# A hybrid decoder step on one core: the first mixer's scan in 8 chunks of 64 tokens instead of 16 of 32

## The chip, the cores and the metric

The kernel runs on one core of a Trainium2 chip. The metric is the device time of one execution in microseconds (us), the median of several runs. The core's engines work side by side, each through its own queue of instructions, and wait for one another on semaphores: PE (TensorE, the matrix multiplications; PEld is its loading of weights), DVE (VectorE), ACT (ScalarE), POOL (GpSimd), and SP (SyncE), which here issues the DMA transfers.

## The reference, cut to what matters

One inference step of a two-layer trunk, for a prompt of 512 new tokens and a sample group of 8 sequences with 4 new tokens each (32 tokens): 544 columns in all. Layer 0 mixes with an RG-LRU and an RWKV-7 side by side, layer 1 with HGRN2, and each is followed by a SwiGLU FFN. The change concerns RWKV-7 alone, which has 8 heads of size 64:

```python
def _rwkv_step(S, inp):
    r_t, w_t, k_t, v_t, kk_t, a_t = inp
    sk = jnp.einsum('bhvk,bhk->bhv', S, kk_t)
    S = (S * w_t[:, :, None, :] - sk[..., None] * (kk_t * a_t)[:, :, None, :]
         + v_t[..., None] * k_t[:, :, None, :])
    return S, jnp.einsum('bhvk,bhk->bhv', S, r_t)
...
    S_T, o = lax.scan(_rwkv_step, S0.astype(F32),
                      (tm(r4), tm(hd(decay)), tm(k4), tm(v4), tm(kk), tm(hd(a))))
    mean = jnp.mean(o, axis=-1, keepdims=True)
    var = jnp.mean(jnp.square(o - mean), axis=-1, keepdims=True)
    on = ((o - mean) * lax.rsqrt(var + GN_EPS)).reshape(B, T, W_B) * lnx_w + lnx_b
    bonus = (jnp.sum(r4 * k4 * r_k, axis=-1, keepdims=True) * v4).reshape(B, T, W_B)
    return (on + bonus) * g, S_T, pb[:, -1]
```

Each token changes a 64x64 state per head by what the token before left, so the step over tokens is a chain. It can be cut into chunks: within a chunk of C tokens the corrections U of all tokens follow from a triangular system of C rows, (I - N) U = rhs, where N holds the products of keys and decayed keys within the chunk and rhs the part that comes from the values V and from the state at the chunk's start. What passes from chunk to chunk is the state alone.

## The kernel before, in words

**The whole.** The program runs mixer 0, its output projection, FFN 0, mixer 1 (HGRN2), its output projection and FFN 1, one after the other. The dense products split each fp32 weight into a high and a low part, `wh` (made by ACT, L202) and `wl` (made by DVE or POOL, L205), and take three products per weight tile on halves of 272 columns. All matrix products go through the helper `mm` (L171), which is why most PE rows of the profile name that line; the tile's name tells them apart (`acc` is a dense product, `ch` the chain of the scan).

**RWKV-7 in chunks of 32.** `NCH` is 16 chunks, `p` counts 4 pairs of heads, `par` the two heads of a pair. `front` and `back` (L542 to L589) make the decayed keys and values factors: `KB` holds both key factors of a chunk (32 columns for V, 32 for U) and `W` the query factors (`al` for the state's part of rhs, the receptance for the output). `scores` (L528) multiplies KB with W, masks the result, and stores it in the other 64 partitions of W: after that one column block of W stacks 64 rows for the state, 32 for V and 32 for U, and one product of 128 rows does all three. The tile `Z` stacks the state S, V and U in the same way. `keys` (L678 to L695) scales KB to KH, turns it with TensorE transposes (tile `tmps`) and ACT copies it to `TM`, which carries V and U to the next state.

**The inverse.** `couple` (L599 to L611) computes N for all chunks, and sends it through DRAM (`nd_p`, the sample's in `nd_s`) so that one partition holds one 32-row block. DVE inverts the two 16-row halves of each block by forward substitution in 15 steps of two instructions (L653, L655). The result Y goes to DRAM (`y_p`) and a transposed copy too (`z_p`), and 16 DMAs bring them back as `Yt` and `Zt` (L670). `join` (L790, L793) builds the lower left quarter of each 32-row block from these with two products per block (tile `jps`), for four chunks at a time.

**The chain.** `scan` (from L803) does per chunk: rhs from W and Z (8 products, tile `ch`), a DVE copy (L827); U from Yt and rhs (8 products), four DVE copies into Z (L842); the new state from TM and Z (8 products), two DVE adds with the decayed state `sp` (L850; `sp` is POOL's, L831); and 8 products for the outputs. The three numbers of `HOP=(8,7,7)` are how many products of other work are placed on PE behind each of these three steps. That other work is the RG-LRU's input projections and gates (L991 to L1050), later the first columns of the output projection (`lead`).

**What sets the order.** The string `MID` orders the last part of the preparation (`a`/`A` and `b`/`B` the two halves of `keys`, `r`/`R` of `receptance`, `x` the values, `g` the output gate). The string `PLAN` orders the scan: `c` a chunk, `s` a stage of the sample group (`sample`, L913 to L985: a scan of its own for the 32 sample tokens, with state products `rpss`, `opss`, `dpss`), `g` and `h` the two halves of the group norm of a block of 128 tokens (L874 to L907), `f` so many products of other work. From the step `r3` on, PE executes in exactly that written order. The queues of the other engines are set when the program is built, by a scheduler with the priorities that the code gives.

```python
    def fill(self, n):
        while n and self.work:
            try:
                next(self.work[0])
                n -= 1
```

Of the kernel before, what the change touches and what calls it, by code (L numbers as in the profile page):

```python
# [30 lines left out]
CH = 32  # L31
HB = CH // 2
NCH = SEQ // CH
EPS = 1e-6
# [17 lines left out]
MID = 'v0 v2 v3 a3 v1 A3 b3 a1 r3 B3 A1 b1 a2 r0 R3 B1 A2 x b2 a0 x r1 x B2 R0 A0 x b0 r2 x R1 B0 g R2'  # L52
# [29 lines left out]
def consts_np():  # L82
# [30 lines left out]
    c["smask"] = np.stack([pair(True), pair(False)], 1)  # L113
    c["upper"] = np.tile((np.arange(CH) < CH // 2)[:, None], (4, 1)).astype(np.float32)
# [14 lines left out]
class Build:  # L129
# [205 lines left out]
    def mixer0(self):  # L335
# [90 lines left out]
        smask = const("smask", [128, 2, 2, 64])  # L426
        upper = const("upper", [128, 1])
        seqsel = const("seqsel", [128, 8])
        block64 = const("block64", [128, 128])
        g2 = const("g2", [128, 512], kp)  # L430

        NC1 = NCH + 1
        W = [[m0.tile([128, NC1, 64], F32, name=f"W{par}{p}") for p in range(4)] for par in range(2)]
        TM = [m0.tile([128, NC1, 64], F32, name=f"TM{p}") for p in range(4)]
# [4 lines left out]
        Yt = m0.tile([128, NCH, 2, CH], F32, name="Yt")  # L439
        Zt = m0.tile([128, NCH, 2, CH], F32, name="Zt")  # L440
        NTt = m0.tile([128, 2, NCH, CH], F32, name="NTt")
        Yts = m0.tile([64, 4, CH], F32, name="Yts")
        sg = kp.tile([128, NT], F32, name="sg")
        nd_p = self.dr.tile([8, NCH, CH, CH], F32, name="nd_p")
        nd_s = self.dr.tile([8, CH, CH], F32, name="nd_s")
        vT = self.dr.tile([NT, 4, 128], F32, name="vT")
        y_p = self.dr.tile([8, NCH, CH, CH], F32, name="y_p")
        z_p = self.dr.tile([8, NCH, CH, CH], F32, name="z_p")
        y_s = self.dr.tile([8, CH, CH], F32, name="y_s")
        par_rows = (slice(0, 64), slice(64, 128))  # L450
        sc_rows = (slice(64, 128), slice(0, 64))
        VS, US = [slice(CH, 64), slice(0, CH)] * 2, [slice(0, CH), slice(CH, 64)] * 2
# [4 lines left out]

        def chunks(z):
            return z.rearrange("p (c t) -> p c t", t=CH)
# [40 lines left out]
        f2 = self.open("feat2")  # L500
        eb = [f2.tile([128, NT + 1], F32, name=f"eb{p}") for p in range(4)]
        KB = [f2.tile([128, NC1, 64], F32, name=f"KB{p}") for p in range(4)]
# [13 lines left out]
        def quarter(c):  # L516
            return slice(32 * (c % 4), 32 * (c % 4) + 32)

        def scores(p):
            for c0, cn in ((0, 8), (8, 8), (16, 1)):  # L520
                ps = self.ms.tile([128, 8, 64], F32, tag="m", name="scps")
                for c in range(c0, c0 + cn):
                    for par in range(2):
                        r = par_rows[par]
                        self.mm(ps[sc_rows[par], c - c0], KB[p][r, c], W[par][p][r, c])
                for par in range(2):
                    sr = sc_rows[par]
                    TT(W[par][p][sr, c0:c0 + cn], ps[sr, 0:cn],  # L528
                       smask[sr, p % 2, c0 // 16, None, :].to_broadcast([64, cn, 64]), OP.mult)
# [27 lines left out]
        def back(p, kap):  # L557
# [23 lines left out]
            E("kb")(KB[p][:, :, VS[p]], chunks(km), chunks(emb), OP.mult)  # L581
            STT(ta, ta, 1.0, kap, op0=OP.add, op1=OP.mult)
            STT(KB[p][:, :, US[p]], chunks(ta), -0.5, chunks(emb), op0=OP.mult, op1=OP.mult)
            for par in range(2):
                r = par_rows[par]
                al = W[par][p][r, :, 0:CH]
                E(f"al{par}")(al, chunks(kap[r]), chunks(eb[p][r, 0:NT]), OP.mult)
                nc.gpsimd.tensor_copy(al[:, 0:NCH, 0:1], kap[r, 0:SEQ:CH][:, :, None])
                nc.gpsimd.tensor_copy(al[:, NCH, 0:CH:NS], kap[r, SEQ::NS])  # L589
# [1098 lines left out]
```

## Time and profile before

| | |
|---|---|
| median of 3 runs | 1540.97 us (1539.78 to 1542.6) |
| profiled execution | 1541.22 us, its span 1539.4 us |
| granted TensorE clock, mean | 0.971 |
| PE busy | 1465.2 us, 95% of the span |
| DVE, ACT, POOL busy | 860.2 us, 552.5 us, 418.3 us |
| mixer 0's preparation and scan | from the start to about 345 us |
| PE idle between 100 and 340 us | 50.5 us (240 us less the busy time of twelve windows of 20 us) |

The profile names engines, lines and tiles: a row of the timeline gives the start in us, the duration, the engine, the line, the operation, output<-input by the program's names, the shape, how many instructions are merged in the row, and in brackets the idle time before it with what ended it. A row of the windows gives for each stretch its length, the busy time of PE, PEld, DVE, ACT and POOL with their numbers of instructions, the granted clock (1.00 is full speed), the share of the DMA engines and GB/s. A row of the waits gives who waited, for whom, and the total us, the number of waits and the longest. A plain fp32 product stands as two instructions on PE: eight products of the program are a row with x16.

### The profile page before, as it was taken

The numbers are of one execution on the slowest core, as the hardware profiler recorded it, in microseconds if no ns is written. First come the engines' busy times: TensorE is split into PE (matmuls) and PEld (weight loads), VectorE is DVE, ScalarE is ACT, GpSimd is POOL, SyncE is SP. The second block draws the span as 40 slices with busy tenths as digits, with TensorE's granted clock in tenths as the row PEclk, the third lists the DMA queues.
The fourth block names the chain that finished last, engine by engine and source line by source line (L and its number), as shares of the span: only waits on it lengthen the run. The fifth ranks groups of instructions, "written<-read, shape, count | busy, mean of one in ns | idle before, by whom it ended". The sixth has DMA issues, their size and how long they took to land.

```text
span 1539.4 us, 33537 instructions
## 1 busy us (share of the span) xinstructions
PE 1465.2 (95%) x13872; PEld 1408.7 (92%) x13872; DVE 860.2 (56%) x1618; ACT 552.5 (36%) x997; POOL 418.3 (27%) x540
## 2 busy tenths in 40 slices
PE   6967888779999999999999999999999999999998
PEld 6857777669999999999999999999999999999997
DVE  7777555785544344334576667666674433444444
ACT  5634234354433233223352333333453322332224
POOL 3664535542110011001133434444431100110010
PEclk9978989889999999999999999999999999999999
DMA  4224311122232322322231232322242222223221
GB/s 158 70 71 104 105 38 36 49 80 93 83 96 83 90 89 84 96 83 91 85 120 58 85 98 85 106 87 90 97 124 90 89 86 87 90 90 90 84 75 59
DMA packets 92010, 133.86 MB, mean 87 GB/s; under 512 B 28976, under 2 KB 34864, under 8 KB 91728
## 3 DMA queue, kind: packets, MB, share of 16 engines
q1 hardware_dynamic: 91856, 131.71, 27.2%
q8 instruction: 109, 1.79, 0.5%
q14 instruction: 45, 0.37, 0.1%
HBM read 120.65 MB, written 11.02 MB: 86 GB/s over the span
## 4 chain that ended last, share of the span: by engine, by line
PE 84%; DVE 7%; ACT 3%; issue 2%; DMA 2%; POOL 1%; SPq 1%; DVEq 0%; POOLq 0%; ACTq 0%
PE acc L171 74%; PE lv L171 2%; PE ops L171 1%; PE ch L171 1%; DVE Z L842 1%; DVE t L571 0%; PE ds L171 0%; PE tr L1503 0%; DVE W L528 0%; PE nps L171 0%; DVE wl L205 0%; DMA S<-rS 0%; DMA x<-xT 0%; DMA wd<-down 0%; DVE Pd L653 0%
## 5 line engine op out<-in xcount | busy, mean ns | idle before, releaser
L171 PE MATMUL acc<-xg,wh 128*128 128x272 f32 x4544 | 888.1, 293 | 11.7 <-ACT xg L262 7.2
L171 PEld LDWEIGHTS acc<-xg,wh 128*128 128x128 f32 x4544 | 721.7, 191 | 21.7 <-ACT xg L262 7.5
L171 PE MATMUL acc<-xg,wl 128*128 128x272 f32 x2272 | 653.1, 293 | 0.2 <-DVE wl L205 0.2
L202 ACT ACTIVATE wh<-wf 128x512 fp32r<-128x512 f32 (+1 forms) x404 | 250.8, 621 | 655.8 <-PE acc L171 544.3
L171 PEld LDWEIGHTS acc<-xg,wl 128*128 128x128 f32 x2272 | 429.1, 190 | 4.9 <-issue 1.3
L205 DVE TENSOR_TENSOR wl<-wf,wh 128x512 fp32r<-128x512 f32 (+1 forms) x373 | 267.1, 716 | 192.2 <-ACT wh L202 166.2
L1207 POOL TENSOR_TENSOR S<-S,rstd 128x272 f32<-128x272 f32 x88 | 74.3, 845 | 645.3 <-ACT S L1206 645.2
L171 PE MATMUL acc<-h,wh 128*128 128x272 f32 x1280 | 236.9, 288 | 0.0
L171 PEld LDWEIGHTS acc<-h,wh 128*128 128x128 f32 x1280 | 198.0, 188 | 0.0
L171 PE MATMUL acc<-h,wl 128*128 128x272 f32 x640 | 176.7, 287 | 0.0
L171 PEld LDWEIGHTS acc<-h,wl 128*128 128x128 f32 x640 | 118.1, 188 | 0.0
L1210 DVE TENSOR_TENSOR hh<-acc,S 128x272 f32<-128x272 f32 x88 | 38.9, 442 | 127.2 <-PE acc L171 125.3
L171 PE MATMUL acc<-cat,wh 128*128 128x272 f32 (+2 forms) x512 | 100.2, 295 | 2.7 <-ACT wh L202 2.7
L171 PEld LDWEIGHTS acc<-cat,wh 128*128 128x128 f32 x512 | 82.7, 194 | 3.5 <-ACT wh L202 3.1
L1206 ACT ACTIVATE S<-t 128x272 f32<-128x272 f32 x88 | 37.8, 431 | 123.4 <-DVE t L1205 123.4
L1227 DVE TENSOR_TENSOR x<-acc,x 128x272 f32<-128x272 f32 x80 | 35.0, 439 | 83.3 <-PE acc L171 83.0
L1205 DVE TENSOR_TENSOR t<-acc,rstd 128x272 f32<-128x272 f32 x88 | 38.7, 441 | 70.7 <-PE acc L171 70.6
L171 PE MATMUL acc<-cat,wl 128*128 128x272 f32 (+2 forms) x256 | 74.2, 296 | 2.0 <-POOL wl L205 1.0
L280 POOL TENSOR_TENSOR ssq<-ssq,sq 128x544 f32<-128x544 f32 x33 | 46.5, 1410 | 93.4 <-ACT sq L279 93.0
L1477 POOL TENSOR_TENSOR K<-K,G 128x256 f32<-128x256 f32 (+1 forms) x48 | 39.8, 828 | 78.3 <-PE lv L171 78.3
L205 POOL TENSOR_TENSOR wl<-wf,wh 128x512 fp32r<-128x512 f32 x31 | 41.3, 1334 | 40.7 <-ACT wh L202 40.4
L171 PEld LDWEIGHTS acc<-cat,wl 128*128 128x128 f32 x256 | 49.2, 194 | 2.8 <-POOL wl L205 1.4
(341 smaller groups left out, 1506.9 us busy)
## 6 DMA issues: line engine op xcount, KB each, us to landing
wf<-gate SPq DMA_DIRECT2D x88, 256.0 KB
wf<-up SPq DMA_DIRECT2D x88, 256.0 KB
wf<-down SPq DMA_DIRECT2D x72, 256.0 KB
wf<-w_in_c SPq DMA_DIRECT2D x64, 256.0 KB
wf<-w_in_ab SPq DMA_DIRECT2D x44, 256.0 KB
x<-xT SPq DMA_DIRECT2D x16, 272.0 KB
wf<-w_out_ab SPq DMA_DIRECT2D x16, 256.0 KB
S<-hS SPq DMA_DIRECT2D x8, 512.0 KB
```

The source lines that it names most:

```text
L171: return self.seq(self.nc.tensor.matmul(out, lhsT, rhs, start=start, stop=stop, skip_group_check=True), chain)
L202: nc.scalar.activation(wh[:, :n], wf[:, :n], AF.Copy)
L205: eng.tensor_tensor(wl[:, :n], wf[:, :n], wh[:, :n].bitcast(F32), OP.subtract)
L280: eng.tensor_tensor(self.ssq, self.ssq, t, OP.add)
L842: nc.vector.tensor_copy(zc[par][q, e::2], cu[q])
L1205: nc.vector.tensor_tensor(t[:, c], ps, rs()[:, c], OP.mult)
L1206: nc.scalar.activation(S[:, c], t[:, c], AF.Silu)
L1207: nc.gpsimd.tensor_tensor(S[:, c], S[:, c], rs()[:, c], OP.mult)
L1210: nc.vector.tensor_tensor(hh[:, c], ps, S[:, c], OP.mult)
L1227: nc.vector.tensor_tensor(x[:, c], ps, x[:, c], OP.add)
L1477: PTT(kv[:, :, 0], kv[:, :, 0], g2[:, :, 1, None].to_broadcast([128, m, b]), OP.mult)
```

## The change

**What it does.** The chunk has 64 tokens instead of 32, so there are 8 chunks instead of 16.

- The stacked tiles go. `W`, `KB`, `TM`, the new `SV` (masked scores for V in the output) and the state `S`, `V`, `U` hold two heads each, one in partitions 0 to 63 and one in 64 to 127, and every product of the chain is 64x64 on one of the two diagonal quadrants of the PE array. What was one product of 128 rows is up to three of 64 rows, added up in PSUM. The masked scores for rhs take the place of KB's first half.
- Per chunk the chain has three steps as before: rhs (8 products with S; the 8 with V stand in the chunk before) and one DVE copy; U (8 products with `T`, the inverse, added to rhs in the same PSUM bank) and one DVE copy; the new state (8 products with U; the 8 with V stand ahead) and one DVE add. 24 products give the outputs. `HOP` is (18,18,18).
- The inverse of 16-row halves stays on DVE. It goes to DRAM as Y alone (the transposed copy and `z_p` go), and 16 DMAs bring it back into the block diagonal of `T`, which POOL has set to zero. `join` then works in two levels, 16 to 32 rows and 32 to 64 rows, in four steps for each group of four chunks; the first group stands in `MID` (four `j`), the second in `PLAN` (`j1` four times).
- `keys` makes one KH of 128x512 for V and one for U, with two buffers, and turns them with 64x64 products against the identity (`turn`) instead of 128x128 transposes; so does the group norm with the outputs.
- The sample's scan keeps blocks of 32 and gets its own tiles (`Ws`, `KBs`, `TMs`). Its stages are now called in groups of three and four (`s3`, `s4` in `PLAN`).
- The pool of the inverse's tiles is opened before the features instead of after them, in other memory.

```diff
-CH = 32
-HB = CH // 2
+CH = 64
+CB = 32
+HB = CB // 2
...
-PLAN = 's1 f30 c1 c1 s1 c1 s1 c1 s1 c1 s1 g0 c1 s1 c1 s1 c1 h0 s1 c1 s1 c1 s1 s1 c1 c1 s1 g1 c1 s1 c1 s1 c1 h1 g2 s1 c1 s1 l3 c1 c1 h2 f20 d0'
+PLAN = 'c1 j1 f12 j1 f8 c1 j1 f4 j1 s1 c1 s1 g0 c1 s3 h0 c1 s4 g1 c1 h1 s4 c1 s3 g2 l3 c1 c1 h2 f20 d0'
...
-HOP = (8, 7, 7)
+HOP = (18, 18, 18)
+KHB = 2
+MIDJ = 4
...
+        iv = self.open("inv", side="right")
+        NTt = iv.tile([128, 4, NCH, CH], F32, name="NTt")
+        Ns = iv.tile([128, CB, CB], F32, name="Ns")
+        Y = iv.tile([128, CB, CB], F32, name="Y")
+        f2 = self.open("feat2", side="right")
...
-            ACT(Zc, Y.rearrange("p i t -> p t i"), AF.Copy)
...
+            for p in range(4):
+                for par in range(2):
+                    for half in range(2):
+                        nc.sync.dma_start(T[quarter(par, half), :, p, CB * half:CB * half + CB],
+                                          y_p[2 * p + par, half::2].rearrange("c i t -> i c t"))
...
+        def turn(out, src):
+            for par in range(2):
+                r = par_rows[par]
+                self.mm(out[r], src[r], ident[r, r])
...
+        def heads(out, w, src, start, stop):
+            for p in range(4):
+                for par in range(2):
+                    r = par_rows[par]
+                    self.mm(out[r, p], w(p)[r], src[r, p], start=start and p == 0, stop=stop, chain=True)
+
+        def outputs(c, V, S, U, ops):
+            for p in range(4):
+                terms = [(SV[p][:, c], V), (W[p][:, c, CH:], S), (KB[p][:, 1, c], U)]
+                if c == 0:
+                    terms.pop(1)
+                for i, (w, x) in enumerate(terms):
+                    for r in par_rows:
+                        self.mm(ops[r, c % 2, p], w[r], x[r, p], start=i == 0, stop=i == len(terms) - 1, chain=True)
...
+                    else:
+                        heads(cr, lambda p: W[p][:, c, 0:CH], S, False, True)
                     nc.vector.tensor_copy(rhs, cr)
+                    heads(cs, lambda p: TM[p][:, 0, c], V, True, False)
...
+                    for p in range(4):
+                        for r in par_rows:
+                            self.mm(cr[r, p], T[r, c, p], rhs[r, p], start=False, stop=True, chain=True)
+                    nc.vector.tensor_copy(U, cr)
                 self.fill(HOP[1])
                 with first():
+                    heads(cs, lambda p: TM[p][:, 1, c], U, False, True)
...
+                    if c + 1 < NCH:
+                        inputs(c + 1)
+                    outputs(c, V, S, U, ops)
```

**How it moves instructions.** On POOL, at the end of the feature preparation, the rows around the first `KH` before are these (`zero` is the tile that clears the sample's block in DRAM, `Y` the inverse's start, `X` the shifted projection):

```order
L476 TENSOR_TENSOR d<-X 128x544
L477 TENSOR_TENSOR d<-shift,X 128x8
L635 MEMSET zero 32x256
L645 MEMSET Y 128x1024
L645 MEMSET Y_1041 64x16
L678 TENSOR_TENSOR KH<-KB_278,ebT 128x512
L681 TENSOR_TENSOR KHs<-KB_278,ebT 128x64
```

and with the change, where the memsets of `zero` and `Y` stand at the very start of the program:

```order
L605 TENSOR_TENSOR bonus<-t_909,bonus 128x544
L617 COPY Ws_258<-kap 64x8
L478 MEMSET X 128x1
L607 TENSOR_TENSOR KBs_262<-bonus,t_924 128x32
L713 TENSOR_TENSOR KHs<-KBs_262,ebT 128x64
L710 TENSOR_TENSOR KH<-KB_250,ebT 128x512 x2
L485 COPY shift_sb<-X 128x9
```

Nothing of the inverse stands ahead of `KH` on POOL any more, and the two KH of a head pair follow one another.

On PE, the end of the sample's scan (`opss` its outputs, `tps` the turned outputs after the group norm, `gps` the output gate, `dpss` its new state). Before, 82 rows of chunks and other work stand between the last `opss` and its `tps`:

```order
L171 MATMUL acc<-xg,wl 128x272
L171 MATMUL acc<-xg,wh 128x272
L895 MATMUL tps<-ident,o 128x32 x4
L171 MATMUL gps<-sg,g_237 128x32 x4
L171 MATMUL ch<-Z_2133,W_239 32x64
L171 MATMUL ch<-Z_2137,W_243 32x64
```

With the change they follow directly, and the later `dpss` of three head pairs stand one behind the other in the same way:

```order
L179 MATMUL opss<-S_3039,am_3044 32x64 x16
L179 MATMUL opss<-Zs_3049,Ws_254 32x64
L179 MATMUL opss<-Zs_3050,Ws_258 32x64
L973 MATMUL tps<-ident,o 128x32 x4
L179 MATMUL gps<-sg,g_241 128x32 x4
L179 MATMUL dpss<-vx,TMs_263 64x512 x2
L179 MATMUL ch<-S,W_243 64x64 x2
```

On DVE, in the middle of the scan (`st`, `o` and `q` are the group norm's, `cf`, `uc`, `ti`, `tr` and `v` the RG-LRU's). Before, these rows stand between one rhs copy and the copies of U into Z, and between these and the adds of the state:

```order
L827 COPY rhs<-ch 128x128
L879 TENSOR_REDUCE st_2830<-q 128x8
L996 TENSOR_TENSOR UX<-acc,rstd 128x240
L998 TENSOR_TENSOR UX<-acc,rstd 128x8x4
L1042 SCALAR_TENSOR_TENSOR tr<-uc,ti 128x544
L881 TENSOR_SCALAR st_2830<-st_2830 128x8
L842 COPY Z_2130<-ch 32x2x64
L842 COPY Z_2134<-ch 32x2x64
```

With the change 29 rows stand between the add of the state of chunk 3 and the copy of rhs of chunk 4, of which these are the last:

```order
L1095 SCALAR_TENSOR_TENSOR uc<-UX,vec,cf 128x512
L1097 SCALAR_TENSOR_TENSOR uc<-UX,vec,cf 128x32
L965 SCALAR_TENSOR_TENSOR st_3780<-st_3780 128x8
L1127 SCALAR_TENSOR_TENSOR v_268<-a,tr 128x544
L963 TENSOR_TENSOR st_3780<-st_3780 128x8
L964 SCALAR_TENSOR_TENSOR st_3780<-st_3780 128x8
L965 SCALAR_TENSOR_TENSOR st_3780<-st_3780 128x8
L963 TENSOR_TENSOR st_3780<-st_3780 128x8
L964 SCALAR_TENSOR_TENSOR st_3780<-st_3780 128x8
L965 SCALAR_TENSOR_TENSOR st_3780<-st_3780 128x8
L907 COPY rhs<-ch 128x256
L917 COPY U<-ch 128x256
```

The work between two copies of the chain is more, and the copies themselves are fewer: 24 instead of 112.

More of the change, by code (lines that the diff above doesn't have):

```diff
@@ L30 @@
 FT = DFF // 128
-CH = 32
-HB = CH // 2
+CH = 64
+CB = 32
+HB = CB // 2
 NCH = SEQ // CH
+NCB = SEQ // CB
 EPS = 1e-6
@@ L683, in keys @@
                         ebT[:, p, NCH:][:, None, :, None].to_broadcast([128, 2, NB, NS]), OP.mult)
             yield
-            ps = self.ms.tile([128, 4, 128], F32, tag="m", name="tmps")
-            for c in range(4):
-                self.seq(nc.tensor.transpose(ps[:, c], KH[:, 2 * c:2 * c + 2].rearrange("p c t -> p (c t)"), ident))
-            for odd in range(2):
-                for par in range(2):
-                    ACT(TM[p][sc_rows[par], c0 + odd:c0 + 8:2], ps[par_rows[odd], :, par_rows[par]], AF.Copy)
@@ L691, in keys @@
-            if half:
+            ps = self.ms.tile([128, NCH, CH], F32, tag="m", name="tmps")
+            for c in range(NCH):
+                turn(ps[:, c], KH[:, c])
+            ACT(TM[p][:, w], ps, AF.Copy)
+            if w:
                 ps = self.ms.tile([64, 128], F32, tag="m", name="tmps")
@@ L731, in mixer0 @@
+        jp = self.open("joins", side="right")
+        joins = itertools.chain(join(0), join(1))
         parts = {}
@@ L763, in mixer0, with load_v, load_vs @@
         self.ms = ms
-        def copy(par, out, src):
-            if par:
-                ACT(out, src, AF.Copy)
-            else:
-                nc.vector.tensor_copy(out, src)
-        def load_v(c, zc):
+        def load_v(c):
+            V = z.tile([128, 4, 64], F32, tag="V", name="V", bufs=nv)
+            for par in range(2):
+                r = par_rows[par]
+                nc.sync.dma_start(V[r], vT[CH * c:CH * c + CH, :, r])
+            return V
+        def load_vs(zc):
             for par in range(2):
@@ L805, in scan, with inputs @@
         def scan():
-            ops = None
-            def slot(c):
-                return [Z[0][c % nz], Z[1][c % nz]]
+            ops = S = None
+            Vs = {}
+            def inputs(c):
+                heads(cr, lambda p: KB[p][:, 0, c], Vs[c], True, c == 0)
             with first():
-                for c in range(nz - 1):
-                    load_v(c, slot(c))
+                for c in range(nv - 1):
+                    Vs[c] = load_v(c)
             yield
-            with first():
-                join(0, 0)
@@ L909, in sample @@
         def sample():
+            for _ in joins:
+                pass
+            if MIDJ < 8:
+                self.close("joins")
             self.close("inv")
@@ L913, in sample @@
             nc.sync.dma_start(S0, I["rS"])
-            am = [sm.tile([128, NB, CH], F32, name=f"am{i}") for i in range(4)]
+            am = [sm.tile([128, NB, CB], F32, name=f"am{i}") for i in range(4)]
             for i in range(4):
@@ L1098, in mixer0 @@
                 self.fill(n)
+            elif k == "j":
+                for _ in range(n):
+                    next(joins, None)
             elif k == "l":
```

345 lines of the change are left out of this document (188 added, 157 removed).

## The prediction

> **What bounds the kernel now.** I read the page first, then the chain, the windows, the waits of PE, and last the timelines at its longest waits. The change stays within mixer 0. Columns of the windows: length, busy time of PE, PEld, DVE, ACT and POOL, granted clock, DMA share, GB/s.
>
> ```profile
> PE 84%; DVE 7%; ACT 3%; issue 2%; DMA 2%; POOL 1%; SPq 1%; DVEq 0%; POOLq 0%; ACTq 0%
> ...
> 100.00:120.00 20.00, 6.24 (x148) 4.93 (x148) 12.35 (x24) 5.55 (x15) 13.38 (x22) 0.57 0.30 83
> 180.00:200.00 20.00, 14.64 (x331) 12.60 (x331) 8.93 (x21) 2.15 (x4) 6.07 (x11) 0.83 0.36 120
> 220.00:240.00 20.00, 17.40 (x288) 14.69 (x288) 13.80 (x41) 4.24 (x9) 10.24 (x15) 0.66 0.08 21
> 260.00:280.00 20.00, 15.19 (x294) 12.87 (x291) 16.39 (x41) 4.73 (x7) 9.48 (x11) 0.83 0.09 23
> 300.00:320.00 20.00, 15.23 (x196) 11.57 (x192) 17.61 (x33) 8.71 (x17) 12.56 (x14) 0.91 0.15 47
> 360.00:380.00 20.00, 20.00 (x157) 20.00 (x156) 11.94 (x16) 9.50 (x15) 6.33 (x4) 1.00 0.09 29
> ```
>
> From 360 us on PE is full at full clock: nothing is to be had there. In mixer 0 it has holes and loses clock: 6.24 busy us at 0.57 before the scan, 15 to 17 us of 20 in the scan. So the time is PE's work in mixer 0, plus what it waits, plus what slow stretches cost. The waits (total, number, longest):
>
> ```profile
> PE ch L171 <- DVE Z L842: 13.9, 11, 3.4
> PE tmps L687 <- POOL KH L678: 10.1, 4, 7.4
> PE rpss L171 <- DMA S<-rS: 3.7, 1, 3.7
> PE tmps L687 <- DVE W L528: 3.6, 1, 3.6
> PE ch L171 <- DVE rhs L827: 3.0, 3, 1.5
> PE tps L895 <- POOL o L889: 1.8, 1, 1.8
> PE tmps L693 <- DVE W L528: 1.4, 2, 1.0
> PE ch L171 <- DVE Z L850: 1.2, 1, 1.2
> ```
>
> The chain waits for DVE 18.1 us (13.9, 3.0, 1.2), the turning of KH for POOL and DVE 15.1 us, the sample's first product for its state 3.7 us.
>
> **A. PE's own work.** One price carries most: 68 instructions (34 products) of 64x64 took 2.20 us, 64.7 ns each.
>
> ```profile
> 147.24 2.20 PE L171 MATMUL scps<-W,KB 64*64 64x64 f32 x68
> 146.60 0.60 PE L687 MATMUL tmps<-ident,KH 128*128 128x128 f32 x4
> 179.99 0.43 PE L171 MATMUL ch<-Z,W 128*32 128x64 f32 x16
> 180.35 0.73 PE L171 MATMUL jps<-Yt,NTt 32*32 32x16 f32 x64
> 105.11 1.77 PE L171 MATMUL ndps<-KB,W 64*32 64x32 f32 x116 [0.30 <-POOL W L588]
> 240.45 0.39 PE L171 MATMUL acc<-xg,wh 128*128 128x272 f32 x1
> 241.83 0.68 PE L171 MATMUL ch<-Z,TM 64*64 64x64 f32 x16 [0.24 <-DVE Z L842]
> ```
>
> - KH turned by 16 products, 1.04 us, instead of a row of 0.60: +0.44, 8 times, +3.5 us. The outputs' turns likewise, 4 times: +1.7.
> - Scores: per pair 16 products of 128 columns at twice the price (2.07) and 18 of 64 (1.16), 3.23 for 2.20: +1.0, 4 times, +4.1. Coupling: +0.2.
> - Joins: 8 rows of 0.73, 5.8 us, become 512 products. At this row's 22.8 ns they take 11.7 us; with half of them, those with 32 columns, at 30.5 ns (1.77 over 58 products, at a clock of 0.50, so an upper bound) 13.6. I take the row of the same shape: +5.8; the other end is +7.8.
> - Chain: 16 times 0.43+0.43+0.68+0.43, 31.5 us, become 496 products of 64.7 ns, 32.1: +0.6. The four steps of a chunk start to start took up to 1 us more than their rows, so +4 is the other end.
> - Between two shapes PE loses time: the 7 products from 240.45 to 241.83 took 1.38 us, of which 0.24 is waiting, where 7 at full rate take 0.86 (162 products in 20 us, 0.1235 each). 0.28 us at each of 48 hops becomes 24 hops: -6.7; below, 0 if the loss goes with the number of shapes.
>
> Sum A: 3.5+1.7+4.1+0.2+5.8+0.6-6.7 = **+9.2**, between +9 and +21.
>
> The Trainium skill ("TensorEngine Tiling (Array Packing)", Instruction Overhead) says that a product carries some 60 cycles, so that one with few columns costs as much as one with 60. By it joins of 32 columns cost what those of 16 do, and the term is its low end, +5.8; with the other end A would be +11.2. No row here has both column counts on 32 rows at one clock.
>
> **B. Waits that go.**
>
> ```profile
> 112.09 0.30 POOL L635 MEMSET zero<- 32x256 f32 x1 [4.28 <-DMA nd_s<-ss]
> 113.30 1.03 POOL L678 TENSOR_TENSOR KH<-KB,ebT 128x512 f32<-128x512 f32 x1
> 114.39 1.12 PE L687 MATMUL tmps<-ident,KH 128*128 128x128 f32 x4 [7.37 <-POOL KH L678]
> ...
> 120.00:125.00 5.00, 5.00 (x30) 5.00 (x29) 4.59 (x13) 1.56 (x5) 1.20 (x1) 0.67 0.07 7
> ```
>
> The first KH stands behind a memset that waits 4.28 us for a transfer, because its tile lies in memory the features just left. With the pool opened earlier that memset and that of the inverse are first in POOL's queue, where nothing waits. A second KH buffer removes the next two waits (1.38 and 1.04). The masks of the scores now stand in the middle of the inversion and not behind it: the 3.6 and 1.0 go. 7.4+1.4+1.0+3.6+1.0 = 14.4, of which I leave 3 for the KH products on POOL (1.03 each): -11.4. The same waits cost clock: three such rows took 1.12 instead of 0.60, and behind them 5 us held 30 products at 0.67 where 40 fit at full clock, 1.3 us lost: together -2.8, or 0 if the clock falls anyway. The state's transfer (3.7) now has a chunk and the joins ahead of its reader: -3.7, and the slow stretch behind it -2.3. The chain's old waits: -18.1. Sum B **-38.3**; the low end -44, the high end -30.
>
> **C. Waits that come.** The chain's DVE work falls from 36.5 us to 10: 24 copies or adds of about 0.42.
>
> ```profile
> L842 DVE COPY Z<-ch 32x128 f32<-32x128 f32 x64 | 18.4, 287 | 10.7 <-PE ch L171 9.7
> L850 DVE TENSOR_TENSOR Z<-ch,sp 64x256 f32<-64x256 f32 x32 | 13.5, 422 | 6.6 <-PE ch L171 5.8
> L827 DVE COPY rhs<-ch 128x128 f32<-128x128 f32 x16 | 4.6, 289 | 14.5 <-PE ch L171 14.3
> ```
>
> But DVE takes its queue in order, and what stood spread over 48 hops stands ahead of 24. Between the add of the state of chunk 3 and the copy of rhs of chunk 4 there are 29 rows, an RG-LRU unit and a group norm. Of the same kind before:
>
> ```profile
> 294.97 0.73 DVE L1044 TENSOR_TENSOR t<-a,h 128x8 f32<-128x8 f32 x1 [0.72 <-ACT a L1036]
> ...
> 307.98 1.28 DVE L1047 TENSOR_TENSOR_SCAN v<-a,tr 128x544 f32<-128x544 f32 x1
> ...
> 292.80 1.28 ACT L1036 ACT_TABLE_LOAD   x1
> ```
>
> By the durations of those rows the 29 take 14.0 us, with some 4.2 us for ACT between them (two table loads of 1.28, and a square and a root that DVE waits for), 18.2 in all. PE has 12 us to do meanwhile: 32 products of the chain, 18 others, the sample's outputs of three pairs, and 8+8+18 of the next step. It waits 6.2. The same count gives 1.9 and 3.2 at chunk 2, 4.5 at chunk 6 and 3 at chunk 7. I drop the last, whose RG-LRU unit can still be late or early by as much: 15.8, between 0 (the queue has drained when the product comes) and 18.6.
>
> The sample's group norm now has no other work on PE between its outputs and their turn. It is a chain of two ACT copies, 16 DVE rows, a square and a POOL product:
>
> ```profile
> L889 POOL TENSOR_TENSOR o<-o,st 32x512 f32<-32x512 f32 x1 | 1.0, 1031 | 0.1
> L976 POOL TENSOR_TENSOR vx<-Zs,seqsel 64x512 f32<-64x512 f32 x8 | 9.7, 1215 | 1.2 <-PE dpss L171 0.7
> ```
>
> 0.75 + 5.6 + 0.9 of ACT and hand-overs + 1.03 = 8.3 us, 1.8 of it paid before: +6.5 (0 to +8). Everything that PE has behind it, two chunks too, waits with it. The three `dpss` in a row each need a `vx` of two POOL rows of 1.215 in one buffer: 1.2+2.6+2.6 = +6.4 (+2 to +8). The first joins read T, which is back from DRAM only after the inversion, one store and 16 loads:
>
> ```profile
> 129.68 0.34 SPq L663 DMA_DIRECT2D y_p<-Y  x1
> 133.39 2.10 SPq L670 DMA_DIRECT2D Yt<-y_p  x4
> ```
>
> There are 16 loads as before; the first reader stood at 180.35 and now stands in the middle of the preparation: +2.5 (0 to +10). The joins' own evictions, a PSUM bank at the second join and a shorter cover of the last group norm: +4.2 (0 to 6). Sum C 15.8+6.5+6.4+2.5+4.2 = **+35.4**, between +10 and +48.
>
> **D. Slow stretches.** In the scan seven times the clock falls to about half for 5 to 13 us. It needs no long gap:
>
> ```profile
> 220.51 0.42 PE L171 MATMUL ch<-rhs,Yt 32*32 32x64 f32 x16 [1.50 <-DVE rhs L827]
> ...
> 223.44 1.12 PE L171 MATMUL ch<-Z,TM 64*64 64x64 f32 x16 [1.44 <-DVE Z L842]
> 225.00:230.00 5.00, 4.35 (x91) 3.45 (x87) 4.88 (x11) 1.07 (x4) 3.96 (x6) 0.50 0.15 42
> 230.00:235.00 5.00, 5.00 (x68) 4.29 (x60) 2.92 (x13) 0.00 (x0) 1.10 (x2) 0.50 0.00 0
> ```
>
> Gaps of 1.50 and 1.44 us, 3 us apart, stood ahead of this one. With four DVE bursts, the sample's norm, the `dpss` and the first join I count seven places again: **0**, from -8 to +6.
>
> **Sum.** +9.2-38.3+35.4+0 = +6.3 on 1541.2 (the profiled execution; the median lies 0.25 under it): **1547 us**.
>
> **The rivals.**
>
> 1. *DVE relieved, faster.* DVE has 26 us less to do in the scan and each hop has 18 products, 2.2 us, as cover for one copy instead of 0.9 for four. If the queue has drained when PE has done its 18 products, the 15.8 falls to 4, and two slow stretches of 3 us go with the gaps: 1547-11.8-6 = **1529**. It decides from where the copies of rhs and U start less than 2.2 us after their product. For it: DVE is busy only 8.9 and 13.8 of 20 us in two of the scan's windows. Against it: 16.4 and 17.6 of 20 in the two with bursts, and the order above.
> 2. *Fewer clock drops, no change.* With 24 hops there are fewer short gaps, and three of the seven places (the joins, the `dpss`, the shortest burst) do not bring the clock down: 6 to 8 us less, **1540**. The Trainium skill ("TensorE: Matmul & The Clock Gate", Part 1) says that the clock halves only after a window of some 3.4 us without work; by that rule only the waits of 4.5, 6.2 and 8.3 us cost clock, and the time is this rival's. The trace is against the rule: the stretch at 223 came without such a gap.
> 3. *T late, slower still.* PE takes its queue in order, so a first join whose T is not there holds all the projections behind it. At the far end, +10 instead of +2.5 and a slow stretch of 3 us more: **1558**.
>
> **How the numbers follow.** The forecast has a chance of 0.34, the first rival 0.30, the second 0.14, the third 0.15; 0.07 is left. This kernel can be told from no change beyond about 0.2%, 3 us. The forecast's own range is 1540 to 1555, so a little of it lies within 3 us, and a part of the second below. Slower 0.48, the same 0.14, faster 0.38. The range takes in the first rival with the 26 us between its bounds halved (1521) and the third with some slow stretches: 1521 to 1564.
>
> **What would show it.** In the profile after: no wait of KH over 2 us and no memset waiting for a transfer near 110 us (B); rows of 64x64 products at 0.5 us for x16 (A); PE waiting for the copies of rhs or U 3 to 6 us at chunks 2, 4 and 6 (C), against none over 1 us (first rival); `tps` of the sample waiting 6 to 8 us; `dpss` 1 to 2.6 us each; the first `jps` under 4 us (against over 8, third rival). The prediction is wrong in its core if the waits of PE between 180 and 340 us add up to less than 20 us, or if 64x64 products on quadrants run at another price than 64.7 ns.

## The result: slower by 3.4%

The changed kernel takes 1593.45 us (1591.88 to 1595.97), the one before beside it 1541.16: a ratio of 1.0341, 95% interval 1.0323 to 1.0359. That is +52 us where +6 was forecast: the right side, outside the range. The page of the profile after (span 1590.1 us, clock 0.963), its chain of waits, and the windows (columns as before):

```profile
PE 1495.7 (94%) x14688; PEld 1441.9 (91%) x14688; DVE 832.9 (52%) x1542; ACT 547.7 (34%) x982; POOL 402.0 (25%) x520
...
PE 78%; DVE 2%; ACT 1%; DMA 1%; POOL 1%; issue 0%; DVEq 0%; POOLq 0%; ACTq 0%; SPq 0%
```

```profile
100.00:120.00 20.00, 16.80 (x255) 15.39 (x255) 13.10 (x30) 4.02 (x11) 15.11 (x20) 0.83 0.28 68
140.00:160.00 20.00, 17.50 (x492) 15.93 (x489) 6.99 (x16) 2.49 (x6) 1.69 (x6) 0.74 0.25 69
180.00:340.00 160.00, 122.21 (x2111) 107.52 (x2111) 67.47 (x146) 52.55 (x86) 53.72 (x79) 0.84 0.16 46
300.00:320.00 20.00, 11.46 (x101) 9.16 (x100) 7.03 (x22) 3.23 (x10) 6.37 (x6) 0.60 0.04 14
340.00:360.00 20.00, 13.75 (x107) 9.51 (x106) 10.85 (x24) 5.36 (x11) 8.57 (x7) 0.67 0.27 93
380.00:400.00 20.00, 8.31 (x139) 7.72 (x136) 10.03 (x27) 5.33 (x12) 1.04 (x1) 0.73 0.50 171
400.00:420.00 20.00, 20.00 (x147) 20.00 (x148) 6.31 (x13) 5.67 (x13) 0.00 (x0) 0.93 0.05 15
```

The span grew by 50.7 us: PE is busy 30.5 us more (1495.7 against 1465.2) and idle 20.2 more. All of it lies in mixer 0: the 100th instruction of its output projection starts at 405.4 us where it started at 353.4, and what follows takes about as long in both, 1185 us. Before that point I weighted each stretch in which PE is busy with its granted clock. By that, 31.3 us were lost to a lowered clock before and 38.6 after, so the growth divides into 23.6 us of more work, 7.3 of lower clock and 21.1 of more idle time.

Between 100 and 120 us it is better: PE is busy 16.80 of 20 us at 0.83 where it was 6.24 at 0.57. But the first product of the chain starts at 193.3 us, not at 180.0, and PE's idle time before it is only 4 us less (30.1 against 34.3). The part that was to gain, the scan, lost: from there to the output projection it takes 212 us instead of 174. From the list of PE's waits in the first 420 us (total, number, longest):

```profile
PE ch L179 <- DVE rhs L907: 14.4, 8, 5.2
PE tps L179 <- POOL o L966: 11.7, 1, 11.7
PE ch L179 <- DVE S L923: 11.3, 6, 6.6
PE dpss L179 <- POOL vx L1056: 7.5, 2, 6.3
PE tps L973 <- POOL o L966: 7.4, 1, 7.4
PE bops L179 <- DVE SV L531: 4.2, 1, 4.2
PE jps L179 <- issue: 3.7, 3, 2.1
PE tmps L179 <- POOL KH L710: 2.2, 1, 2.2
PE ch L179 <- DVE S L925: 1.3, 1, 1.3
```

The chain waits 27.0 us for DVE (14.4, 11.3, 1.3) where it waited 18.1, though DVE is busy 67.47 us between 180 and 340 us where it was busy 107.78; this is the row of before for it:

```profile
180.00:340.00 160.00, 128.97 (x2166) 105.54 (x2166) 107.78 (x267) 67.11 (x112) 72.84 (x91) 0.88 0.19 58
```

This window holds less of the scan than it did before. From the first product of the chain to the output projection DVE is busy 96.8 us, where it was 119.1.

Two group norms (the sample's, L973, and the prompt's last, 11.7 us), the `dpss`, the `bops` and the first joins are new or longer.

The timeline of PE after, at some of these places:

```profile
209.54 0.68 PE L179 MATMUL ch<-S,W 64*64 64x64 f32 x16
210.75 0.68 PE L179 MATMUL ch<-V,TM 64*64 64x64 f32 x16 [0.53 <-DVE rhs L907]
...
217.78 0.68 PE L179 MATMUL ch<-U,TM 64*64 64x64 f32 x16
219.06 0.68 PE L179 MATMUL ch<-V,KB 64*64 64x64 f32 x16 [0.60 <-DVE S L923]
...
229.76 1.12 PE L179 MATMUL ch<-V,TM 64*64 64x64 f32 x16 [3.40 <-DVE rhs L907]
...
283.08 1.12 PE L179 MATMUL ch<-V,TM 64*64 64x64 f32 x16 [5.19 <-DVE rhs L907]
...
362.64 1.12 PE L179 MATMUL ch<-V,KB 64*64 64x64 f32 x16 [6.56 <-DVE S L923]
...
397.93 1.97 PE L179 MATMUL tps<-ident,o 64*64 64x64 f32 x32 [11.69 <-POOL o L966]
```

Here is what I had overlooked. rhs and the state's sum are the two halves of one tile `ch`. The V products that feed them (`ch<-V,TM`, and for the next chunk `ch<-V,KB`) stand on PE directly behind the products whose result DVE is to fetch, and each starts only when DVE's fetch from `ch` is done. Even with DVE free this costs 0.53 and 0.60 us; with rows ahead of the fetch in DVE's queue it costs all of them. The 18 products of other work stand behind the V products, so they cover the copy of U and nothing else.

The fifteen waits for rhs and the state are of two kinds. Four long ones, at chunks 2, 4 and 6 (3.40 and 5.19 us for rhs, 2.36 and 6.56 for the state), make 17.5 of the 27.0 us. The other eleven, of 0.5 to 1.5 us each, make 9.5.

### The profile page after: what moved, and what is told of

The parts are those of the page before. It is cut to its first block, busy times and chain, and to the rows that moved or that the text cites. A ratio compares the mean times of both kernels' runs of the same rounds, so it can differ in the third digit from the quotient of the medians.

```text
span 1590.1 us, 34915 instructions
## 1 busy us (share of the span) xinstructions
PE 1495.7 (94%) x14688; PEld 1441.9 (91%) x14688; DVE 832.9 (52%) x1542; ACT 547.7 (34%) x982; POOL 402.0 (25%) x520
## 4 chain that ended last, share of the span: by engine, by line
PE 78%; DVE 2%; ACT 1%; DMA 1%; POOL 1%; issue 0%; DVEq 0%; POOLq 0%; ACTq 0%; SPq 0%
PE acc L179 70%; PE lv L179 2%; PE ops L179 1%; PE ch L179 1%; DMA wf<-w_out_ab 1%; PE dpss L179 0%; PE ds L179 0%; PE tr L1586 0%; PE gps L179 0%; PE nps L179 0%; PE opsm L179 0%; PE d L179 0%; PE opsq L179 0%; DMA x<-xT 0%; PE gate L179 0%
## 5 line engine op out<-in xcount | busy, mean ns | idle before, releaser
L1289 ACT ACTIVATE S<-t 128x272 f32<-128x272 f32 x88 | 37.8, 431 | 122.5 <-DVE t L1288 122.5
```

What stands on the lines that cost most here:

```text
L1289: nc.scalar.activation(S[:, c], t[:, c], AF.Silu)
```

## The experiments

All ratios are to the kernel before, run beside it; 0.01 is 15.4 us.

### The joins

`e_nojoin` is the change without the joins, `b_nojoin` the kernel before without its own.

```diff
-            pa = self.ms.tile([128, 4, 4, HB], F32, tag="m", name="jps")
...
-                    copy(par, T[a, 4 * g + odd:4 * g + 4:2, :, CB:], ps[odd][a])
-            yield
+            for _ in range(4):
+                yield
```

> The change without any of the work of the joins: the products, evictions and waits of both groups are left out, so the inverse keeps only its 16-row blocks and the outputs of the first mixer are not the reference's. Theory WORK: the joins cost 13 us of PE work and about 7 us of waits and gaps, none of it hidden; 1593 becomes about 1575. Rival (the joins fill holes that are there anyway, since the chain waits for DVE right after): 1588 to 1593. GROUPING says nothing of it.

> The kernel before without any work of its joins (the first mixer's outputs are not the reference's). Its joins are 5 us of PE work in the trace: 1540 becomes 1533 to 1537. If they lie in the chain's waits for DVE: 1538 to 1541.

`e_nojoin`: 1554.41 us, 1.0098 (1.0085 to 1.0111), a larger gain than either theory had. `b_nojoin`: 1537.58 us, 0.9985 (0.9976 to 0.9995). The joins of two levels cost 2.4%, 37 us; those of one level cost 2. In the trace without them (to the same point, as above) PE's work is 11.9 us less, the loss by clock 12.0 less, the idle time 14.1 less. The window at the first joins with the joins (first) and without (second fence):

```profile
144.00:146.00 2.00, 1.78 (x137) 1.56 (x131) 1.75 (x5) 0.00 (x0) 0.00 (x0) 1.00 0.76 221
146.00:148.00 2.00, 0.80 (x59) 0.69 (x54) 0.00 (x0) 0.00 (x0) 0.00 (x0) 0.72 0.56 206
148.00:150.00 2.00, 2.00 (x88) 1.81 (x80) 0.48 (x1) 0.60 (x1) 0.00 (x0) 0.50 0.03 9
154.00:156.00 2.00, 1.76 (x9) 1.67 (x9) 0.09 (x1) 0.38 (x1) 0.00 (x0) 0.50 0.04 11
```

```profile
140.00:160.00 20.00, 20.00 (x260) 18.91 (x256) 12.01 (x27) 3.98 (x8) 8.79 (x28) 1.00 0.53 153
```

With the joins PE stands 1.20 us (146.1 to 147.3). The clock falls within that gap, at 146.9 us, and stays at 0.50 until 157.1; without the joins PE is busy all 20 us at full clock. In the kernel before the joins filled time in which PE waited anyway: without them its work is 4.6 us less and its idle time 3.6 more.

`e_joinsep` issues the products with NTt and those with the identity in two runs instead of in turn, to tell whether mixing them is what costs. `e_joinmid` puts the four first joins later in the preparation, so that T has time to come back.

```diff
-... R0 j x j r2 x j R1 j B0 g R2'
+... R0 x r2 j x j R1 j B0 j g R2'
```

> The change with one thing altered: in the first and the third step of each join the products of the two kinds, which alternate in the change (16 columns with the N blocks, 32 columns against the identity), stand as two runs of one kind each; the same products in all. Theory SHAPES (the alternation makes PE wait for its own issue, 3.7 us in the trace, and drops its clock for 10 us each time): the issue waits of the joins fall under 1 us and 1593 becomes 1578 to 1585. Rival SUPPLY (so many short products run faster than PE is given instructions, whatever their order): the issue waits stay and the time is 1590 to 1596.

> The change with one thing altered: the four steps of the first join stand later in the preparation, the first of them 48 products later, so that T is back from DRAM and each step has other work behind it. Theory LATE T (part of the joins' 39 us is that the first one waits for T and for DVE, and that the clock falls behind these waits): its waits of about 5 us and the slow stretch of 10 us behind go, 1593 becomes 1580 to 1586. Rival (the waits are PE's own at so many short products, wherever they stand): 1590 to 1596.

`e_joinsep`: 1593.81 us, 1.0354 (1.0328 to 1.0379): the mixing costs nothing. Its trace puts part of the first wait on T: `PE jps` waits 2.5 us for the transfer from `y_p`. `e_joinmid`: 1580.74 us, 1.0274 (1.0255 to 1.0293): the place is worth 10 us. But that is not time saved in the joins: PE's idle time ahead of `jps` is 7.2 us there and 7.3 in the change. What fell are the waits ahead of `ch` (21.0 us instead of 27.1) and the loss by clock (34.9 instead of 38.6). So the run does not show what a late T costs. The gaps stay, though T's last transfer is issued at 141.9 us and the first `jps` starts at 148.0:

```profile
152.28 0.21 PE L179 MATMUL jps<-ident,T 32*32 32x32 f32 x1 [2.09 <-issue]
156.89 0.83 PE L179 MATMUL jps<-jp,jz 32*32 32x16 f32 x46 [1.48 <-issue]
```

"issue" is time in which PE waited for nothing that the profile shows. The transfers that load instructions are denser at the joins; the list of DMA queues from 143 to 157 us (queue, packets, MB, share) has for the kernel before and then for the change:

```profile
q8 instruction: 1, 0.02, 0.7%
```

```profile
q8 instruction: 4, 0.07, 2.0%
```

Queue q8 carries one packet of 16 KB for some 255 instructions of PE and PEld in both kernels (109 packets for 27744, 115 for 29376), so I take it to be PE's. The packets tell more. The change and its ten versions with joins have 36 gaps of 0.35 us or more before 420 us that are put down to "issue". Every one of them ends 1.25 to 1.67 us after such a packet has arrived. Of the 303 waits of that length for a named releaser, 13 end 1.2 to 1.7 us after one. The three versions without these joins have no such gap, nor has the kernel before. That PE waited for its instructions to be loaded is what the traces point to. No run varied the loading, so it is not shown by experiment.

### The sample's stages in groups

`e_spread` calls the sample's stages one at a time between the three steps of a chunk (two more `yield`s), `b_coarse` groups them in the kernel before like in the change. `b_coarse` also leaves out the store of the prompt's final state.

```diff
 e_spread
-PLAN = 'c1 j1 f12 j1 f8 c1 j1 f4 j1 s1 c1 s1 g0 c1 s3 h0 c1 s4 g1 c1 h1 s4 c1 s3 g2 l3 c1 c1 h2 f20 d0'
+PLAN = 'c1 j1 f12 j1 f8 c3 j1 f4 j1 s1 c1 s1 c1 s1 c1 g0 c1 s1 c1 s1 c1 s1 h0 c1 s1 c1 s1 c1 s1 g1 c1 s1 c1 s1 c1 h1 c1 s1 c1 s1 c1 s1 g2 l3 c1 s1 c1 s1 c1 c3 h2 f20 d0'
...
                 self.fill(HOP[0])
+                yield
...
                 self.fill(HOP[1])
+                yield
 b_coarse
+PLAN = 's1 f30 c1 c2 c2 s1 g0 c2 s3 h0 c2 s4 g1 c2 h1 s4 c2 s3 g2 l3 c4 h2 f20 d0'
```

> The change with one thing altered: the sample's sixteen stages stand one by one behind the steps of the chunks (at most one per step) instead of in groups of three and four; the products, the chunks of 64 and the joins are as in the change. Theory GROUPING (most of the loss is that nothing stands on PE between the dependent stages of the sample, and that the stores of its state hold up the loads of the output projection's weights on SP): the wait of the sample's turned outputs falls from 7.4 to under 3 us, those of its state products from 7.5 to under 2, the add of the state's 6.6 and part of the last norm's 11.7 go; 1593 becomes about 1568. Theory WORK (64x64 products on quadrants and joins in two levels are some 20 us more of PE work, and bursts of DVE the rest): 1585 to 1595.

> The kernel before (chunks of 32) with one thing altered: the sample's stages are called in the groups and at the places of the change (three, four, four and three at a time). Theory GROUPING: the waits that the change shows at the sample (7.4 and 7.5 us) and at the late weights (6.6 us and part of 11.7) appear here too; 1541 becomes about 1560. Rival WORK (the groups do not matter, the shape of the products does): 1539 to 1545.

`e_spread`: 1575.76 us, 1.0235 (1.0221 to 1.025), 16 us less than the change. `b_coarse`: 1555.23 us, 1.0106 (1.0093 to 1.0119), 16 us more than before. So the grouping costs the same in both. From the waits of `e_spread`:

```profile
PE ch L179 <- DVE rhs L907: 19.2, 8, 6.4
PE tps L179 <- POOL o L968: 12.0, 1, 12.0
PE ch L179 <- DVE S L925: 11.6, 6, 4.0
PE tps L975 <- POOL o L968: 1.9, 1, 1.9
```

The sample's norm falls from 7.4 to 1.9 and `dpss` is gone from the list, but the chain waits 5 us more: the stages had been no burden of the chain's waits. `e_nojoin_spread` is both:

> Both alterations at once: the sample's stages one by one behind the steps of the chunks, and the joins left out (the first mixer's outputs are not the reference's). Theory JOINS + GROUPING (the two are separate losses of 39 and 18 us, and nearly all of the 52): they add, 1593 becomes 1534 to 1540, no slower than the kernel before. Rival (both free the same holes of PE, so that they overlap): 1546 to 1552.

1540.44 us, 0.9997 (0.9981 to 1.0014). The two gains, 2.43 and 1.06 points, add up (3.44 together), and the change is level with the kernel before.

### The chain's waits for DVE

`e_nolru` leaves out the RG-LRU's recurrence, most of DVE's bursts. `e_hop12` is `e_spread` with `HOP=(12,12,12)`: less other work per step, more kept for the end. `e_cover` moves the V products behind the other work.

```diff
 e_cover
-                    if c == 0:
-                        inputs(0)
-                    else:
+                    inputs(c)
+                    if c:
                         heads(cr, lambda p: W[p][:, c, 0:CH], S, False, True)
                     nc.vector.tensor_copy(rhs, cr)
-                    heads(cs, lambda p: TM[p][:, 0, c], V, True, False)
...
                 self.fill(HOP[0])
                 with first():
+                    heads(cs, lambda p: TM[p][:, 0, c], V, True, False)
...
-                    if c + 1 < NCH:
-                        inputs(c + 1)
                     outputs(c, V, S, U, ops)
```

> The change without the RG-LRU's recurrence: its exponentials, squares, roots, their DVE rows and the scan are left out for all four units (one add stands for them, and the RG-LRU's outputs are not the reference's); convolution, gates and products stay. Theory BURSTS (DVE rows of RG-LRU units and their ACT round trips ahead of the copies of the chain make PE wait): the waits of the chain for DVE fall from 27 to 10 us or less, and 1593 becomes 1572 to 1580. Rival (the group norms and the low parts of the activations do it): the waits stay over 18 us and the time is over 1585.

> The change with the sample's stages spread as before, and 12 instead of 18 other products behind each step of a chunk, so that some 140 of them are left for the end of the scan. Theory TAIL (the last group norm waits 12 us for want of other products, since the chunks have used them up): that wait falls under 3 us, the chain's own waits grow by less than 6, and 1576 becomes 1566 to 1572. Rival COVER (the 18 products hide the DVE work between the steps): the chain's waits grow from 32 to 45 us or more and the time is 1576 to 1590.

> The change with one thing altered in the chain: the products of V with KB and of V with TM, which stand directly behind the step whose result DVE still has to fetch from the same PSUM bank, stand behind the 18 other products instead; the same products in all. Theory NO COVER (the fetches of rhs and of the state have nothing ahead of their next writer, so that each costs 0.5 to 0.6 us and every DVE row ahead of it in full): the chain's waits for DVE fall from 27 to about 10 us, the clock falls less often, and 1593 becomes 1568 to 1578. Rival SERIES (DVE, ACT and POOL are a chain of their own that sets the pace, so that a wait removed here comes back at the next step): 1586 to 1594.

`e_nolru`: 1578.06 us, without an interval. This single run is 15 us under the change, as the theory of the bursts had it, but not for its reason: the chain still waits 22.3 us of 27.0, so the RG-LRU's rows in DVE's queue are not the main thing. In its trace PE's idle time is 10.0 us less, of which 3.9 lie at `dpss`, and the loss by clock 4.3 less. `e_hop12`: 1583.06 us, 1.0283 (1.0249 to 1.0316), 7 us more than `e_spread`, with intervals that just touch. The time is in the range of COVER, but its reason is not borne out: the chain's waits fell to 23.5 us, where it had 45 or more. The wait of the last group norm is gone, but PE now waits for the RG-LRU's gates and the output projection's input, and its idle time is 78.7 us against 80.0.

`e_cover`: 1562.21 us, 1.0148 (1.0129 to 1.0168), 30 us less than the change, with the same instructions on PE in another order. From its waits:

```profile
PE tps L179 <- POOL o L963: 12.3, 1, 12.3
PE tps L970 <- POOL o L963: 7.4, 1, 7.4
PE ch L179 <- DVE U L916: 5.6, 2, 4.7
PE dpss L179 <- POOL vx L1053: 4.8, 3, 2.6
```

27.0 us of waiting for rhs and S became 5.6 for U; with the 18 products ahead of the V products, the long waits are covered like the short ones. The rest of the gain is clock: 30.6 us lost to it instead of 38.6. The other engines have the same instructions too, DVE's in an order that differs at 67 of 1542 places. No run gave rhs and the state's sum a tile each. With the stages spread as well:

> The same alteration of the chain together with the sample's stages spread one by one. NO COVER and GROUPING as separate losses: 1576 becomes 1550 to 1560. SERIES: 1568 to 1577.

1554.56 us, 1.0096 (1.0081 to 1.0112): 37.8 us under the change, where the two alone make 46. The losses overlap in part.

### The change repaired

`e_all` is `e_cover_spread` with the joins at `e_joinmid`'s place. The last group norm still waits 10.1 us there: the first `HOP` steps use up the products that could stand ahead of it. `e_fit46` and `e_fit42` are `e_all` with 46 and 42 products per chunk, `HOP=(16,16,14)` and `(15,15,12)`; `e_all_nojoin` is `e_all` without the joins.

> All three alterations: the chain's products behind the other work, the sample's stages one by one, the first join later. If the three losses are separate: 1542 to 1552, the joins' 12 us of PE work being what is left. SERIES: 1560 to 1570.

> The version with all three alterations, and 16, 16 and 14 products behind the steps instead of 18 each, so that about 64 more are left behind the last chunk (83 instead of 19). Theory TAIL (the last group norm waits 10 us for want of products, now that the chain does not need 18 for cover): that wait falls under 4 us, the chain's waits stay under 8, and 1552 becomes 1540 to 1546. Rival UNIT (the RG-LRU's last unit, whose products then come later, takes its place as the last chain, as with 12 products): 1550 to 1556.

> As the run before with 15, 15 and 12 products, about 96 more behind the last chunk. TAIL: no wait of the last group norm at all, 1538 to 1545. UNIT: the gates of the RG-LRU's last unit wait over 5 us and the time is 1552 to 1560.

> The version with all three alterations without any work of the joins (the first mixer's outputs are not the reference's). If the joins cost their PE work of 12 us and some 5 us of waits and clock: 1552 becomes 1532 to 1538. If they cost 30 us or more here too, as they did in the change: 1518 to 1524. If they only fill holes: 1546 to 1552.

| | us | ratio (95%) |
|---|---|---|
| the change | 1593.45 | 1.0341 (1.0323 to 1.0359) |
| `e_all` | 1552.24 | 1.0085 (1.0068 to 1.0102) |
| `e_fit46` | 1537.2 | 0.998 (0.9966 to 0.9994) |
| `e_fit42` | 1545.76 | 1.0038 (1.0023 to 1.0054) |
| `e_all_nojoin` | 1522.31 | 0.9886 (0.9868 to 0.9905) |

`e_fit46` is the fastest kernel that computes all, 0.2% under the one before, at the edge of what can be told. From its waits:

```profile
PE acc L179 <- ACT xg L270: 6.9, 1, 6.9
PE jps L179 <- issue: 6.5, 4, 2.4
PE acc L179 <- ACT cat L265: 6.3, 1, 6.3
PE tps L972 <- POOL o L965: 5.8, 1, 5.8
PE ch L179 <- DVE U L917: 2.0, 1, 2.0
PE ch L179 <- DVE rhs L906: 1.6, 1, 1.6
```

The wait ahead of the last group norm is gone and the chain waits 3.6 us; 6.3 us for the output projection's input (`cat`) have come, and the joins' gaps of 6.5 remain. The optimum is narrow: with four products fewer per chunk the median is 9 us longer. The wait at the sample's group norm (L972) is then 10.7 us instead of 5.8, but the two profiled executions differ by 0.8 us only, so the traces do not show what the 9 us are.

The joins cost 31 us even here (1.0085 to 0.9886). Without joins on either side the larger chunk is faster by 1.0%, 15 us (0.9886 against 0.9985). So the change without its joins is faster, and the inverse of 64 rows costs twice what is gained. How much of the 15 us is the chunk's alone is not shown: `e_all_nojoin` has the three other alterations too, and the kernel before was not reworked in the same way.

### The first KH

`b_prep` is the kernel before with `zero` a small tile set at the start, so that no memset stands ahead of the first KH and waits for a transfer.

```diff
+        zero = kp.tile([128, 64], F32, name="zero")
+        nc.gpsimd.memset(zero, 0.0)
...
-            zero = iv.tile([32, 8, CH], F32, name="zero")
-            nc.gpsimd.memset(zero, 0.0)
```

> The kernel before with one thing altered: the memory that clears the sample's block in DRAM is a small tile of its own, set to zero at the start, so that the memset ahead of the first KH on POOL no longer waits 4.3 us for a transfer. If the prediction's term for it is right, the wait of 7.4 us shrinks to about 3 and 1541 becomes 1535 to 1537. Rival (the inversion, which ends later, or the memset of Y behind it takes its place): 1540 to 1542.

1538.71 us, 0.9998 (0.9987 to 1.0008): nothing gained. In its trace the longest wait for KH fell from 7.4 to 3.3 us, one for W grew from 3.6 to 5.0, and all of PE's idle time in mixer 0 fell by 1.7 us.

## Why the prediction was wrong, by its steps

The sum was 45.7 us short: 14.4 in PE's own work (+9.2 forecast, +23.6 measured), 18.9 in PE's idle time (+2.2 forecast, +21.1 measured) and 12.4 in the clock (-5.1 forecast, the 2.8 and 2.3 of B; +7.3 measured).

**A, PE's own work: +9.2 forecast, +23.6 measured,** beyond its upper end of +21. Each group's time from one start to the next, at full clock, gives:

- Joins +7.8, the upper end, but for two other reasons than columns. "512 products" was a wrong count: there are 576 (1152 instructions of tile `jps`). They took 12.7 us, 22.0 ns each, where 22.8 was forecast; those before took 4.9, not 5.8, since their rows overlap. What 32 columns cost against 16 is seen in `e_joinsep`, which has long rows of each at a granted clock of 1.00:

```profile
162.17 0.86 PE L179 MATMUL jps<-T,NTt 32*32 32x32 f32 x59
182.07 1.39 PE L179 MATMUL jps<-T,NTt 32*32 32x16 f32 x126 [1.21 <-DVE bonus L754]
161.20:163.00 1.80, 1.80 (x133) 1.55 (x131) 0.34 (x1) 1.43 (x3) 1.39 (x3) 1.00 0.51 146
182.00:183.60 1.60, 1.53 (x139) 1.38 (x139) 0.36 (x2) 0.00 (x0) 0.61 (x1) 1.00 0.64 138
```

  Less the 0.18 us that one instruction alone shows, that is 11.7 ns an instruction with 32 columns and 9.7 with 16: a fifth more. The Trainium skill ("TensorEngine Tiling (Array Packing)", Instruction Overhead), by which both would cost the same, is nearer to these two rows than the third more of the prediction's other end, but not met. Two other rows of 32 columns in that trace, also at full clock, took 14.7 ns (44 instructions at 183.34 us) and 17.3 ns (64 at 168.37), so the number of columns is not all that sets the price.
- Chain and outputs +7.8, forecast +0.6. The 496 products took 34.4 us, 69 ns each, near the 64.7. The step that failed most is the other side: "16 times 0.43+0.43+0.68+0.43, 31.5 us". Rows of PE overlap, and from start to start the old chain took 26.6.
- KH +3.8 (3.5 forecast), the outputs' turns +2.2 (1.7), scores +2.4 (4.1), coupling +2.0 (0.2), fewer changes of shape -6.2 (-6.7): small errors that cancel. These groups add up to 19.8. The other 3.8 us are spread; 2.6 of them lie on the sample's `opss`, `rpss` and `dpss`, whose numbers are the same as before and which the prediction left out.

**B, waits that go: held in the trace, less in the time.** The waits for KH fell from 10.1 us to 2.2, the state's 3.7 are gone, and the turning of KH waits no longer for the masks of the scores. But PE waits for those masks elsewhere now: 4.2 us at `bops` and 2.1 in the joins, for DVE's L531, where the prediction struck out 4.6. And `b_prep` took away the memset that held the first KH, and the time did not move; that a wait is gone does not say that its length is won.

**C, waits that come: +35.4 forecast.** (Its bounds of +10 and +48 are not those of its terms, which add up to +2 and +50.6.) Two sizes were about right: the sample's norm +5.6 (7.4 less 1.8 paid before; forecast 6.5) and `dpss` 7.5 (6.4, though as one wait of 6.3 and one of 1.2, not three). `e_spread` and `b_coarse` show that the grouping as a whole costs some 16 us. Two others were not right:

- "PE has 12 us to do meanwhile" is the step that failed in the chain. The last of what it counts, the V products and the 18 others of the next step, stands behind the fetch and cannot run during it. The waits were 27.0 us and not 15.8. The bursts themselves came at the chunks that were named, with 17.5 us for the forecast 15.8, a closeness that owes something to luck, since part of the cover was not there. What had been put at nothing are the other eleven fetches, 9.5 us. `e_cover` shows the cause: the same instructions in another order on PE are 30 us faster, clock included.
- The cover of the last group norm stood, with the joins' evictions and a bank, at +4.2. It waits 11.7 us: behind the last chunk PE had 22 instructions of other work where 65 had stood. `e_fit46` takes the wait away.

**The joins' waits and clock: the largest miss.** They stood in three terms, work +5.8, T +2.5 and a part of 4.2, some 10 us, and cost 37 where those before cost 2. Work was the smallest part of the error. The gaps that the profile puts on "issue" were in no term, and the half clock was one of seven places that D counted and took for equal: the traces put 12.0 us of the joins' cost on the clock and 14.1 on idle time, of which 7.3 lie ahead of the joins' own products. In all the loss by clock rose by 7.3 us, a little over D's upper bound of +6, and the 5.1 us that B took off for it did not come. One reading in D was not right: the clock of the kernel before fell at 222.2 us, inside the gap of 1.44 us and not behind it.

**The rivals.** The first, DVE relieved, fell, though its condition nearly held: all eight copies of U and six of the eight of rhs start less than 2.2 us after their product. PE waited none the less, since its next products stand directly behind the fetches of rhs and of the state. With the order repaired the chain's part of it comes true: the chain waits 3.6 us in `e_fit46`. The second fell: the loss to the clock rose. The third fell by its own sign: the first join of the change waits 0.4 and 1.2 us, neither of them put down to T. T does hold it in some versions (2.5 us in `e_joinsep`). That `e_joinmid` gets 10 us back, about what this rival added to the forecast, is chance: the idle time in the joins is the same there.

The two signs by which the prediction called itself wrong in its core did not show: PE was idle 37.8 us between 180 and 340 us (more than 20), and 64x64 products ran at about their price.

**Open** is what PE waits for inside the joins. The arrival of its instructions fits every gap, but no run shows it. Of the 31 us that the joins cost in `e_all`, the traces with and without them put 13.4 on work, 5.4 on the clock and 8.8 on idle time (27.6, where the profiled executions differ by 28.0).

## What to carry to other kernels

Before counting work as cover, look at which instruction stands directly behind the one whose result is fetched: if it needs the same tile, it waits for the fetch, and what stands after it covers nothing. When a chain is made shorter, ask which other work gets coarser with it (here an inverse of one more level and stages in groups), and price that with its gaps and clock, not only with its products. Durations of rows that overlap must not be added; take them from start to start.

## What the runs showed of the hardware

- Inside dense runs of very small products, or just behind them, PE stood 0.4 to 2.7 us with no releaser that the profile names. Each such gap, 36 in eleven traces, ended 1.25 to 1.67 us after a packet of the instruction queue q8 had arrived.
- The clock read 0.50 for 10 us (146.9 to 157.1) after a gap of 1.20 us had begun. The Trainium skill ("TensorE: Matmul & The Clock Gate", Part 1) has the clock fall only after some 3.4 us without work; here it fell 0.8 us into that gap, and the only other long gap in the 3.4 us before was one of 0.41 us.
- The order of products on PE, with the same instructions, was worth 30 us (`e_cover`), though DVE was busy only 67.47 of 160 us.
- Mixing products of 16 and 32 columns on the 32x32 tiles costs nothing against running them apart (1.0354 against 1.0341, with intervals that overlap).
